# Gate and branch products with tokens on partitions, and a new order at the two ends of a two-block network

## The chip, the cores and the metric

The kernel runs on one core of a Trainium2 chip. The metric is device time in microseconds, from start to end of one execution. Three runs of the kernel before gave 2169.39, 2167.85 and 2166.99 us; their median is 2167.85 us. Beside them there is one execution recorded by the hardware profiler.

The core has five engines with queues of their own: TensorE (PE in the profile; its weight loads are PEld), VectorE (DVE), ScalarE (ACT), GpSimd (POOL) and SyncE (SP), which here issues most DMA transfers. Products land in PSUM; everything else that engines work on lies in SBUF.

## The reference

256 tokens of width 1024 pass through a first block and then through two layers of a second one. All is float32. What matters here, in short:

```python
# block 1
proj = rmsnorm(x) @ w_in                       # q, f, i, g, attention q, k, v, gates
y_hg = hgrn2_mix(...) @ w_branch_hg            # 1024 x 1024
y_at = moba_attention(...) @ w_branch_attn     # 1024 x 1024
gates = sigmoid(gl.reshape(B, S, 2, D))
merged = gates[:, :, 0] * y_hg + gates[:, :, 1] * y_at
x = x + merged @ w_out
x = x + (silu(h2 @ w_gate) * (h2 @ w_up)) @ w_down

# block 2, two layers (the first with a dense feed-forward, the second with 8 experts, top 2)
z = xn @ w_in[layer]
gates = sigmoid(z[..., OFF_GATE:].reshape(b_, s_, 4, D))
merged = (gates[:, :, 0] * (y_a @ w_branch_pool)    # 256 x 1024
          + gates[:, :, 1] * (y_b @ w_branch_conv)  # 256 x 1024
          + gates[:, :, 2] * (y_c @ w_branch_sgu)   # 256 x 1024
          + gates[:, :, 3] * (y_d @ w_branch_attn)) # 512 x 1024
h = h + merged @ w_out
```

## The kernel before

**Products.** A float32 operand is split into a rounded part `hi` and the rest `lo` (both fp32r), and a product is made of three matmuls, hi x hi, hi x lo and lo x hi. Weights come from HBM in `raw` buffers (seven of 128x2048). A *piece* is a part of a buffer with up to 1024 columns per partition; `look_ahead` (L383) copies it to `hi` on ACT, and the subtraction that gives `lo` (L408) is issued on DVE one unit later. Three pieces are split ahead (`LOOK`), with four buffers each for `hi` and `lo`.

**Units and side work.** `unit` (L460) is the step by which everything is ordered. It calls the generators of side work once (`stage`), issues the products of one piece, calls `look_ahead`, then `flush` (which issues the evacuation left by the unit before, and deferred work), and calls the same generators a second time (`finish`). So a side generator makes two calls per unit; only the first `width` of the list `sides` are served. `drain` serves side work without products between. The order on each engine is the order of the calls.

**Layouts.** `chunk_t` (L497) computes 256 output columns with the weights as stationary operand and the 256 tokens as moving one: output columns on partitions, 256 columns per matmul. `chunk_wide` (L549) has the activations as stationary operand and 512 weight columns as the moving one: tokens on partitions, two token halves `t`, 512 columns per matmul.

**Gates and branches of block 1.** Eight `chunk_t` give the gates (`evac_gate`, L842: DVE scales by the norm). Then, for each of eight groups of 128 output columns, there are two units of 24 matmuls (`o` with w_branch_hg, `att` with w_branch_attn), and `evac_merge` (L851) multiplies by the gate, adds the two and calls `merge_split` (L867), which splits the sum into the `hi` and `lo` operand `merged` of w_out.

**Gates and branches of a mixer.** The attention (`diff`, two chains of side work), `sgu`, `pool` and `conv` run as side work while 16 `chunk_t` compute the gates (L1334). `drain` (L1337) ends them all. Then, per group of 128 output columns, come a unit with w_branch_attn (12 matmuls) and one with the three smaller branches (18 matmuls). `evac_merge` (L1340) multiplies two pages of gates by the products on DVE; for the first six groups POOL makes the two additions, for the last two DVE. `merge_split` follows one or two units later.

**After them.** `residual` (L874) multiplies `merged` by w_out; its first chunk is `chunk_late` (L506), which leaves the last two of eight row groups to the end, since `merged` comes last there. The second layer goes to `moe` (L1370) instead, whose products with w_out begin with `chunk_tok_pair` (L567).

**Weights.** `plan_all` (L351) lists all pieces in order. `fill` (L367) issues loads on SP as buffers come free. Entries marked `RAW` use a raw buffer; `ANY` may also take four pages of the pool of 50 pages of 128x512, as many as `room` allows (in mixer 1 set to `ROOM_MERGE` ahead of the branches).

**PSUM.** There are two pools of four banks: `psg` for the main products (`gp`) and `pss` for side work (`sp`).

**The two ends.** `first_chunk` (L639) loads the input and the first weights in eight steps and multiplies at once. `overflow` (L1540) is a second pass over the experts for the case that one expert has more than 128 tokens; here it isn't entered. It is a conditional block at the end of the program, in which every engine branches:

```python
with self.tc.If(self.n_longest > P, preferred_fallthrough_block=False):
```

With `True` the body is to be placed next in the program, with `False` the other arm, and without the argument the compiler selects.

Of the kernel before, what the change touches and what calls it, by code (L numbers as in the profile page):

```python
# [126 lines left out]
class Net:  # L127
# [160 lines left out]
    def plan_block1(self):  # L288
# [15 lines left out]
        for c in range(8):  # L304
            yield from t(7168, c)
        for c in range(4):
            yield RAW
            p0 = self.load(a["w_branch_hg"][0], 0, 8, 256 * c, 256)
            yield RAW
            p1 = self.load(a["w_branch_attn"][0], 0, 8, 256 * c, 256)  # L310
            for m in range(2):
                yield p0[:, :, m * P:m * P + P], m
                yield p1[:, :, m * P:m * P + P], m
# [4 lines left out]
    def plan_mixer(self, l):  # L318
# [8 lines left out]
        for c in range(4):  # L327
            for b in range(4):
                yield from self.plan_t(w, 3072 + 1024 * b + 256 * c, 8)
        for c in range(4):  # L330
            yield RAW
            v = self.load(a["w_branch_attn_2"][l], 0, 4, 256 * c, 256)
            yield RAW
            raw = self.rawp.tile([P, 2048], F32, tag="raw", name=self.nm("raw"))[:, :1536].rearrange("p (k c) -> p k c", k=6)
            for i, nme in enumerate(("w_branch_pool_2", "w_branch_conv_2", "w_branch_sgu_2")):
                self.nc.sync.dma_start(raw[:, 2 * i:2 * i + 2, :], a[nme][l][:, 256 * c:256 * c + 256].rearrange("(k p) c -> p k c", p=P))
            for m in range(2):
                yield v[:, :, m * P:m * P + P], m
                yield raw[:, :, m * P:m * P + P], m
# [208 lines left out]

    def chunk_wide(self, x, evacs, width=1):  # L549

        mm = self.nc.tensor.matmul
        ps = [[self.gp() for _ in range(2)] for _ in evacs]

        def products(ps, hi, lo, r):
            for t in range(2):
                s = slice(t * P, t * P + P)
                for k in range(2):
                    xh, xl = self.xb(x, r + k)
                    mm(ps[t], xh[:, s], hi[:, k, :], start=r + k == 0, stop=False)  # L559
                    mm(ps[t], xl[:, s], hi[:, k, :], start=False, stop=False)  # L560
                    mm(ps[t], xh[:, s], lo[:, k, :], start=False, stop=r + k == 7)  # L561
        for q in range(0, 8, 4):
            for p, evac in zip(ps, evacs):
                for r in (q, q + 2):
                    self.unit(lambda hi, lo: products(p, hi, lo, r), (lambda p=p, evac=evac: evac(p)) if r == 6 else None, width)

    def chunk_tok_pair(self, x, evacs, width=1):  # L567

        ps = [[self.gp()[:, :256] for _ in range(2)] for _ in range(2)]
        for r in (0, 4):  # L570
            for i in range(2):
                self.unit(lambda hi, lo: self.mm3tok(ps[i], hi, lo, x, r),
# [66 lines left out]
    def first_chunk(self, N, xr, evac):  # L639
# [4 lines left out]
        for i in range(4):  # L644
            nc.sync.dma_start(self.x[i], xr[i])
            v = w[2 * P * i:2 * P * i + 2 * P, 1024:1536].rearrange("(k p) c -> p k c", p=P)
            for k in range(2):
                (nc.sync if i + k else nc.scalar).dma_start(raws[i // 2][:, 2 * (i % 2) + k, :], v[:, k, :])
# [7 lines left out]
        for i in range(4):  # L656
# [25 lines left out]
    def setup(self):  # L682
        nc, a, const = self.nc, self.a, self.const
        self.params = const.tile([P, NPAR], F32, name="params")
        nc.scalar.dma_start(self.params, a["params"])
# [50 lines left out]
    def block1(self):  # L736
# [74 lines left out]
        for c in range(4):  # L811
# [16 lines left out]
            if c == 1:  # L828
                self.side(bias[1])
        aq, ak, av = [None] * 4, [None] * 4, [None] * 4  # L830
# [9 lines left out]
        gates = [self.pgv(2, T, nm="gl") for _ in range(8)]  # L840

        def evac_gate(c, ps):  # L842
            b, m = divmod(c, 4)
# [986 lines left out]
```

## Time and profile before

| | |
|---|---|
| median of three runs | 2167.85 us |
| the profiled execution, whole time | 2167.5 us |
| its span, from first to last instruction | 2165.6 us |
| instructions | 35720 |
| HBM read, written | 558.32 MB, 4.75 MB |
| branch matmuls of block 1 | from 264.6 to about 310.8 us |
| branch matmuls of mixer 0 (tile b) | from 699.8 to about 730.8 us |
| branch matmuls of mixer 1 (tile b) | from 1123.9 to about 1154.9 us |
| the experts | from about 1199 to 2157 us |

A line of a group reads: line of the source, engine, operation, output<-inputs by the program's names, form, count, and then busy time and mean, or min/median/max in ns. A line of the chain or of a timeline begins with start and length in us. `[0.83 <-DVE gt L1342]` is idle time before an instruction and what ended it. [...]

### The profile page before, as it was taken

How to read it: one execution, taken by the hardware profiler on the slowest of the kernel's cores; microseconds unless marked ns; L12 is line 12 of the kernel's file. 1: busy time of each engine (PE TensorE's matmuls, PEld its weight loads, DVE VectorE, ACT ScalarE, POOL GpSimd, SP SyncE). 2: the span in 40 equal slices, each digit the busy share in tenths (PEclk: the TensorE clock that was granted, in tenths of full speed). 3: DMA queues.
4: the chain of work that ended last, by engine and by line, in shares of the span. 5: the costliest groups of instructions: out<-in, count | busy, mean ns of one | idle time of the engine just before them, and what ended most of it. 6: DMA issues, size and time to landing. Idle time of an engine off the chain costs nothing.

```text
span 2165.6 us, 35720 instructions
## 1 busy us (share of the span) xinstructions
PE 2144.1 (99%) x13587; PEld 1938.1 (89%) x13587; DVE 1769.9 (82%) x2513; ACT 1424.0 (66%) x2015; POOL 101.0 (5%) x114
## 2 busy tenths in 40 slices
PE   9999999999999999999999999999999999999998
PEld 9988999999999999999998888888888888888886
DVE  7877766655787976557878999989999999999997
ACT  6347555444655554446555888888887888788885
POOL 0000000003000300020012000000000000000100
PEclk9999999999999999999999999999999999999999
DMA  9444466646543755474548799999999999999994
GB/s 346 141 136 156 130 193 185 186 159 222 192 157 110 230 186 171 160 243 156 166 132 306 274 323 387 364 357 379 369 377 367 384 374 385 345 383 371 387 386 168
DMA packets 368275, 565.48 MB, mean 261 GB/s; under 512 B 14378, under 2 KB 177210, under 8 KB 368096
## 3 DMA queue, kind: packets, MB, share of 16 engines
q1 hardware_dynamic: 363600, 551.50, 73.4%
q0 software_dynamic: 4064, 11.05, 1.4%
q8 instruction: 108, 1.77, 0.3%
q14 instruction: 71, 0.58, 0.1%
q10 hardware_dynamic: 432, 0.57, 0.1%
HBM read 558.32 MB, written 4.75 MB: 260 GB/s over the span
## 4 chain that ended last, share of the span: by engine, by line
PE 95%; DVE 2%; DMA 1%; issue 0%; SPq 0%; ACT 0%; ACTq 0%; DVEq 0%
PE g L493 13%; PE g L494 13%; PE g L495 13%; PE g L1656 9%; PE g L1658 9%; PE g L1657 9%; PE y L1679 5%; PE y L1680 5%; PE y L1681 5%; PE g L559 2%; PE g L561 2%; PE g L560 2%; PE lev L990 1%; PE at L1636 1%; DVE lo L408 1%; PE xe L1575 1%
## 5 line engine op out<-in xcount | busy, mean ns | idle before, releaser
L185 ACT ACTIVATE hi<-raw 128x1024 fp32r<-128x1024 f32 (+2 forms) x1236 | 1125.7, 927 | 582.7 <-PE g L494 278.4
L408 DVE TENSOR_TENSOR lo<-raw,hi 128x1024 fp32r<-128x1024 f32 (+1 forms) x1228 | 1282.0, 1071 | 205.4 <-ACT hi L185 170.9
L493 PE MATMUL g<-nh,hi 128*128 128x256 f32 x1664 | 476.7, 286 | 0.0
L494 PE MATMUL g<-nl,hi 128*128 128x256 f32 x1664 | 471.1, 283 | 0.0
L495 PE MATMUL g<-nh,lo 128*128 128x256 f32 x1664 | 471.1, 283 | 0.0
L1656 PE MATMUL g<-hi,xe 128*128 128x512 f32 x896 | 354.0, 395 | 0.0
L1658 PE MATMUL g<-lo,xe 128*128 128x512 f32 x896 | 349.5, 390 | 0.0
L1657 PE MATMUL g<-hi,xe 128*128 128x512 f32 x896 | 349.2, 390 | 0.0
L493 PEld LDWEIGHTS g<-nh,hi 128*128 128x128 f32 x1664 | 319.2, 192 | 3.4 <-issue 2.3
L494 PEld LDWEIGHTS g<-nl,hi 128*128 128x128 f32 x1664 | 319.4, 192 | 0.3
L495 PEld LDWEIGHTS g<-nh,lo 128*128 128x128 f32 x1664 | 319.2, 192 | 0.0
L1658 PEld LDWEIGHTS g<-lo,xe 128*128 128x128 f32 x896 | 168.2, 188 | 35.8
L1657 PEld LDWEIGHTS g<-hi,xe 128*128 128x128 f32 x896 | 168.5, 188 | 33.4
L1656 PEld LDWEIGHTS g<-hi,xe 128*128 128x128 f32 x896 | 168.4, 188 | 33.4
L1679 PE MATMUL y<-hi,ah 128*128 128x512 f32 x448 | 175.9, 393 | 0.0
L1680 PE MATMUL y<-hi,al 128*128 128x512 f32 x448 | 174.6, 390 | 0.0
L1681 PE MATMUL y<-lo,ah 128*128 128x512 f32 x448 | 174.5, 390 | 0.0
L1681 PEld LDWEIGHTS y<-lo,ah 128*128 128x128 f32 x448 | 84.1, 188 | 17.7
L495 PE MATMUL g<-ah,lo 128*128 128x256 f32 x352 | 99.7, 283 | 0.0
L493 PE MATMUL g<-ah,hi 128*128 128x256 f32 x352 | 99.7, 283 | 0.0
L494 PE MATMUL g<-al,hi 128*128 128x256 f32 x352 | 99.7, 283 | 0.0
L1679 PEld LDWEIGHTS y<-hi,ah 128*128 128x128 f32 x448 | 84.2, 188 | 16.6
(427 smaller groups left out, 2809.3 us busy)
## 6 DMA issues: line engine op xcount, KB each, us to landing
raw<-in_moe_w_gate_up_dram SPq DMA_DIRECT2D x168, 1024.0 KB, 7.0
raw<-in_w_in_dram SPq DMA_DIRECT2D x90, 1024.0 KB, 5.2
raw<-in_moe_w_down_dram SPq DMA_DIRECT2D x88, 1024.0 KB, 6.1
raw<-in_moe_w_gate_up_dram SPq DMA_DIRECT2D x224, 256.0 KB, 7.3
raw<-in_moe_w_down_dram SPq DMA_DIRECT2D x96, 256.0 KB, 7.0
raw<-in_ffn_w_gate_up_dram SPq DMA_DIRECT2D x22, 1024.0 KB, 5.2
raw<-in_w_ffn_gate_dram SPq DMA_DIRECT2D x11, 1024.0 KB, 5.4
raw<-in_w_ffn_up_dram SPq DMA_DIRECT2D x11, 1024.0 KB, 5.3
```

The lines of the kernel that those rows point to most:

```text
L185: return self.nc.scalar.activation(out, in_, func, **kw)
L408: self.nc.vector.tensor_sub(l, x, h)
L493: mm(out, hi[:, k, :], xh, start=r + k == 0, stop=False)
L494: mm(out, hi[:, k, :], xl, start=False, stop=False)
L495: mm(out, lo[:, k, :], xh, start=False, stop=r + k == kb - 1)
L559: mm(ps[t], xh[:, s], hi[:, k, :], start=r + k == 0, stop=False)
L1656: mm(ps, xh, hi[:, k, :], start=first, stop=False)
L1657: mm(ps, xl, hi[:, k, :], start=False, stop=False)
L1658: mm(ps, xh, lo[:, k, :], start=False, stop=last)
L1679: mm(py, xh, hi[:, i, :], start=k == 0, stop=False)
L1680: mm(py, xl, hi[:, i, :], start=False, stop=False)
L1681: mm(py, xh, lo[:, i, :], start=False, stop=k == KE - 1)
```

## The change

Gates and branches are computed by `chunk_wide` or in its manner (`products_tok`), 512 output columns at a time. The gates are scaled on ACT while they leave PSUM. Products are multiplied and added on DVE (`gated`) with tokens on partitions; the sum is transposed on PE (`turn`) and split from PSUM (`merge`, `merge_now`). In block 1 the order is gates, then branches by halves of the columns. In a mixer, six of the eight wide gate chunks come first; the other two (gates 2 and 3 of the second half) are cut into half chunks and put between the branches of the first half. `sgu`, `pool` and `conv` go to the front of the side work. The last branch's multiplication is issued at once, and its merge inside the first products with w_out (`between`, `chunk_late_pair`, `chunk_tok_pair`). The loads follow the new order.

At the start, the first weight load leads ACT's queue ahead of `params`, `x[0]` is loaded in halves, later weights in one transfer of two row groups, and the first `hi` copy goes to DVE. At the end, `preferred_fallthrough_block` is left out.

```diff
 def plan_block1(self):
-        for c in range(8):
-            yield from t(7168, c)
...
+            yield from self.plan_wide(w, [7168 + 512 * (c // 2) + 1024 * (c % 2)])
+        for c in range(2):
+            for nme in ("w_branch_hg", "w_branch_attn"):
+                yield from self.plan_wide(a[nme][0], [512 * c])
 def plan_mixer(self, l):
...
+        gates = [[g for b in range(4) for g in self.plan_loads(w, 3072 + 1024 * b + 512 * c)] for c in range(2)]
+        branches = [self.plan_branches(l, c) for c in range(2)]
+        for g in gates[0] + gates[1][:5] + [branches[0][0], gates[1][5], branches[0][1], gates[1][6], branches[0][2], gates[1][7]] + branches[1]:
+            yield from g
...
+    def products_tok(self, ps, hi, lo, x, r, kb):
+        mm = self.nc.tensor.matmul
+        for t in range(2):
+            s = slice(t * P, t * P + P)
+            for k in range(2):
+                xh, xl = self.xb(x, r + k)
+                mm(ps[t], xh[:, s], hi[:, k, :], start=r + k == 0, stop=False)
+                mm(ps[t], xl[:, s], hi[:, k, :], start=False, stop=False)
+                mm(ps[t], xh[:, s], lo[:, k, :], start=False, stop=r + k == kb - 1)
+
+    def chunk_late_pair(self, x, evacs, between):
+        ps = [self.gp()[:, :T] for _ in range(4)]
+        late = []
+        for i in range(4):
+            if i == 2:
+                between()
+            run = self.stage(1)
+            late.append(self.ahead.pop(0))
+            self.mm3t(ps[i], *late[i], x, 0, 4, 8)
+            if i == 0:
+                self.look_ahead()
+            elif i == 1:
+                self.rest()
+                self.rest = lambda: None
+            self.flush()
+            self.finish(run)
+        for i, (hi, lo) in enumerate(late):
+            self.mm3t(ps[i], hi[:, 4:, :], lo[:, 4:, :], x, 4, 4, 8)
+            self.look_ahead()
+            self.flush()
+            if i % 2:
+                self.pending.append(lambda i=i: evacs[i // 2](ps[i - 1:i + 1]))
...
 def first_chunk(self, N, xr, evac):
         for i in range(4):
-            nc.sync.dma_start(self.x[i], xr[i])
             v = w[2 * P * i:2 * P * i + 2 * P, 1024:1536].rearrange("(k p) c -> p k c", p=P)
+            dst = raws[i // 2][:, 2 * (i % 2):2 * (i % 2) + 2, :]
+            if i:
+                nc.sync.dma_start(self.x[i], xr[i])
+                nc.sync.dma_start(dst, v)
+                continue
             for k in range(2):
-                (nc.sync if i + k else nc.scalar).dma_start(raws[i // 2][:, 2 * (i % 2) + k, :], v[:, k, :])
+                nc.sync.dma_start(self.x[i][:, k, :], xr[i][:, k, :])
+                (nc.sync if k else nc.scalar).dma_start(dst[:, k, :], v[:, k, :])
+        nc.scalar.dma_start(self.params, self.a["params"])
...
-                self.copy(hi[:, k, :], v[:, k, :])
+                if i + k:
+                    self.copy(hi[:, k, :], v[:, k, :])
+                else:
+                    nc.vector.tensor_copy(hi[:, k, :], v[:, k, :])
...
+    def evac_gate(self, gates, c, ps, N, func=AF.Copy):
+        gates[c] = [self.pg(nm="gt") for _ in range(2)]
+        for t, g in enumerate(gates[c]):
+            self.act(g, ps[t], func, scale=N.col[:, t:t + 1])
+
+    def gated(self, gates, b, c, ps):
+        for t in range(2):
+            g = gates[b][c][t]
+            self.nc.vector.tensor_mul(g, g, ps[t])
+            if b != self.first_branch:
+                s = gates[self.first_branch][c][t]
+                self.nc.vector.tensor_add(s, s, g)
+
+    def evac_branch(self, gates, b, c, ps, merged):
+        self.gated(gates, b, c, ps)
+        if b == self.last_branch:
+            self.side(self.merge(gates, c, merged), front=True)
+
+    def turn(self, gates, c, j):
+        pt = self.sp("mt").rearrange("p (k t) -> p k t", k=2)
+        for t in range(2):
+            y = gates[self.first_branch][c][t]
+            for k in range(2):
+                self.nc.tensor.transpose(pt[:, k, t * P:t * P + P], y[:, (2 * j + k) * P:(2 * j + k) * P + P], self.ident)
+        return pt
...
+    def merge_now(self, gates, c, merged):
+        pts = [self.turn(gates, c, j) for j in range(2)]
+        for j, pt in enumerate(pts):
+            hi, lo = merged[2 * c + j] = tuple(self.pgv(2, T, dt=F32R, nm="m" + s) for s in "hl")
+            self.copy(hi, pt)
+            self.nc.vector.tensor_sub(lo, pt, hi)
...
 def mixer(self, l, N, S):
+        for b in range(4):
+            self.chunk_wide(N.x, [lambda ps, b=b: self.evac_gate(gates[b], 0, ps, N)], width=2)
+        for b in range(2):
+            self.chunk_wide(N.x, [lambda ps, b=b: self.evac_gate(gates[b], 1, ps, N)], width=2)
+        self.drain(gens=small)
+        todo = [(b, 0) for b in range(4)] + [(b, 1) for b in range(2)]
+
+        def gate_half(b, r, width=2):
+            if r == 0:
+                late[b] = [self.gp() for _ in range(2)]
+            for q in (r, r + 2):
+                self.unit(lambda hi, lo: self.products_tok(late[b], hi, lo, N.x, q, 8),
+                          (lambda: self.evac_gate(gates[b], 1, late[b], N, AF.Sigmoid)) if q == 6 else None, width)
...
+        def branch(b, c, evac=True):
+            x = (ya, yb, yc, yd)[b]
+            ps = [self.gp() for _ in range(2)]
+            n = 4 if b == 3 else 2
+            for r in range(0, n, 2):
+                self.unit(lambda hi, lo: self.products_tok(ps, hi, lo, x, r, n),
+                          (lambda: self.evac_branch(gates, b, c, ps, merged)) if evac and r == n - 2 else None)
+            return ps
...
+        gate_half(2, 0)
+        self.drain()
+        sigmoids(2)
+        branch(0, 0)
+        sigmoids(1)
+        branch(1, 0)
+        gate_half(2, 4, 1)
+        sigmoids(1)
+        branch(2, 0)
+        gate_half(3, 0, 1)
+        sigmoids(1)
+        branch(3, 0)
+        gate_half(3, 4, 1)
+        sigmoids(1)
+        for b in range(3):
+            branch(b, 1)
+        ps = branch(3, 1, False)
+        self.flush()
+        self.gated(gates, 3, 1, ps)
+        return merged, lambda: self.merge_now(gates, 1, merged)
...
 def overflow(self):
-        with self.tc.If(self.n_longest > P, preferred_fallthrough_block=False):
+        with self.tc.If(self.n_longest > P):
```

`sigmoids(n)` applies the sigmoid on ACT to the two pages of each of the next n entries of `todo`. `merge` does what `merge_now` does, as side work.

More of the change, by code (lines that the diff above doesn't have):

```diff
@@ L571, in chunk_tok_pair @@
             for i in range(2):
+                if r == 0 and i == 1:
+                    between()
                 self.unit(lambda hi, lo: self.mm3tok(ps[i], hi, lo, x, r),
@@ L862, in block1 @@
-        self.flush(True)
-        N = self.residual(merged, 8, self.par("g_ffn", 8))
+        for c in range(2):
+            for b, x in enumerate((o, att)):
+                for g in gates[b][c]:
+                    self.act(g, g, AF.Sigmoid)
+                ps = [self.gp() for _ in range(2)]
+                for r in range(0, 8, 2):
+                    last = r == 6 and not (b and c)
+                    self.unit(lambda hi, lo: self.products_tok(ps, hi, lo, x, r, 8),
+                              (lambda b=b, c=c, ps=ps: self.evac_branch(gates, b, c, ps, merged)) if last else None)
@@ new lines, in merge @@
+    def merge(self, gates, c, merged):
+        for j in range(2):
+            yield 1
+            yield 1
+            pt = self.turn(gates, c, j)
+            yield 1
+            hi, lo = merged[2 * c + j] = tuple(self.pgv(2, T, dt=F32R, nm="m" + s) for s in "hl")
+            self.copy(hi, pt)
+            self.defer(lambda pt=pt, hi=hi, lo=lo: self.nc.vector.tensor_sub(lo, pt, hi))
+            yield 1
+    def merge_now(self, gates, c, merged):
+        pts = [self.turn(gates, c, j) for j in range(2)]
+        for j, pt in enumerate(pts):
+            hi, lo = merged[2 * c + j] = tuple(self.pgv(2, T, dt=F32R, nm="m" + s) for s in "hl")
+            self.copy(hi, pt)
+            self.nc.vector.tensor_sub(lo, pt, hi)
@@ new lines, in mixer, with sigmoids @@
+        self.drain(gens=small)
[6 more added lines that the diff above has]
+                          (lambda: self.evac_gate(gates[b], 1, late[b], N, AF.Sigmoid)) if q == 6 else None, width)
+        def sigmoids(n):
+            for _ in range(n):
+                if todo:
+                    b, c = todo.pop(0)
+                    for g in gates[b][c]:
+                        self.act(g, g, AF.Sigmoid)
@@ L1352, in mixer @@
+        def branch(b, c, evac=True):
+            x = (ya, yb, yc, yd)[b]
+            ps = [self.gp() for _ in range(2)]
+            n = 4 if b == 3 else 2
[3 more added lines that the diff above has]
+            return ps
+        late = {}
         if l:
@@ L1414, in moe @@
         evacs = [lambda ps, c=c: evac(c, ps) for c in range(4)]
[L1415 removed]
+        self.chunk_tok_pair(merged, evacs[:2], between, width=4)
         for c in range(2, 4):
@@ L1758, in run @@
             self.side(st)
-            merged = self.mixer(0, N, S)
-            N = self.residual(merged, 8, self.par(("n2", 0), 8))
+            merged, between = self.mixer(0, N, S)
+            N = self.residual(merged, 8, self.par(("n2", 0), 8), between)
             N = self.ffn(N, self.par(("n1", 1), 8))
@@ L1765, in run @@
             self.side(self.res_tok())
-            merged = self.mixer(1, N, S)
-            self.moe(merged)
+            merged, between = self.mixer(1, N, S)
+            self.moe(merged, between)
             self.overflow()
```

139 lines of the change are left out of this document (40 added, 99 removed).

## The prediction

> **What bounds the kernel now.** I read the head of the page first, then the chain that ended last, then windows of single stages.
>
> ```profile
> PE 2144.1 (99%) x13587; PEld 1938.1 (89%) x13587; DVE 1769.9 (82%) x2513; ACT 1424.0 (66%) x2015; POOL 101.0 (5%) x114
> PEclk9999999999999999999999999999999999999999
> PE 95%; DVE 2%; DMA 1%; issue 0%; SPq 0%; ACT 0%; ACTq 0%; DVEq 0%
> ```
>
> TensorE's clock is granted throughout, and the chain is PE for 95%. So an edit is worth what it does to the count and spacing of products, to the few places where PE is starved, or to the two ends. PE's busy share hides short gaps, because products overlap; gaps are found by counting products in a window. In these rows the second number is the length in us, and after it stand busy us and count of each engine:
>
> ```profile
> 264.60:310.90 46.30, 46.30 (x388) 46.30 (x387) 29.54 (x38) 25.84 (x33) 0.00 (x0) 1.00 0.61 195
> 346.00:526.00 180.00, 180.00 (x1496) 179.84 (x1497) 111.32 (x121) 83.56 (x96) 12.84 (x17) 1.00 0.59 187
> 699.96:739.90 39.94, 35.91 (x290) 34.86 (x288) 38.50 (x48) 23.68 (x41) 16.56 (x12) 1.00 0.74 231
> 1124.00:1161.00 37.00, 33.10 (x269) 32.23 (x268) 35.68 (x45) 22.22 (x41) 16.59 (x12) 1.00 0.97 330
> ```
>
> The second row, 1496 products of 256 columns in 180 us, gives 0.120 us each. The first is the branch stage of block 1: 388 x 0.120 = 46.6, so PE never waits there. Rows three and four are the branch stages of the two mixers with the first products after them: 290 x 0.120 = 34.8 of 39.9 us, and 269 x 0.120 = 32.3 of 37.0. PE loses 5.1 and 4.7 us. The 55 longest pieces of the chain say to whom, and the groups of tile gt, at 690 to 745 us, say why (min/median/max ns):
>
> ```profile
> 714.60 1.44 DVE ml L872
> 719.17 1.51 DVE ml L872
> 723.90 1.43 DVE ml L872
> 728.54 1.43 DVE ml L872
> L872 DVE TENSOR_TENSOR ml<-gt,mh x8: 418/1510/1522, 709.9 to 738.4; 128x256 fp32r<-128x256 f32 x8
> L1345 POOL TENSOR_TENSOR gt<-gt,gt x6: 1887/1914/1942, 705.4 to 727.8; 128x512 f32<-128x512 f32 x6
> L1342 DVE TENSOR_TENSOR gt<-gt,b x8: 673/675/680, 704.0 to 735.4; 128x512 f32<-128x512 f32 x8
> L1345 DVE TENSOR_TENSOR gt<-gt,gt x2: 691/692/693, 732.9 to 736.7; 128x512 f32<-128x512 f32 x2
> L185 ACT ACTIVATE gt<-gt x16: 611/616/632, 698.9 to 722.2; 128x512 f32<-128x512 f32 x16
> PE b L493 <- DVE gt L1342: 3.3, 4, 0.8
> ```
>
> One output column of 128 takes 4.65 us ((728.54 - 714.60)/3) where its 30 products take 3.6. DVE is the bound: the subtraction ml takes 1.51 us while POOL adds, 0.42 without. PE then waits for the multiplication L1342 that must free its PSUM bank.
>
> **The change part by part.** First the wider products. Two stretches of the old 512-wide stages, in the projections (0.2267 = 1.36/6) and in the experts, where four transposes stand between:
>
> ```profile
> 171.41 0.39 PE L561 MATMUL g<-lo,nh 128*128 128x512 f32 x1
> 172.77 0.39 PE L561 MATMUL g<-lo,nh 128*128 128x512 f32 x1
> ...
> 1341.43 0.60 PE L1636 MATMUL at<-consts,s 128*128 128x128 f32 x4
> 1341.78 0.48 PE L1656 MATMUL g<-hi,xe 128*128 128x512 f32 x1
> 1342.10 0.40 PE L1657 MATMUL g<-hi,xe 128*128 128x512 f32 x1
> ```
>
> A pair of 256-wide products (0.2400) becomes one of 512 (0.2267): 0.0133 us less. Block 1 has 8 gate chunks x 48 + 8 columns x 48 = 768 products, hence 384 pairs: -5.1 us. A mixer has 16 x 48 + 8 x 30 = 1008, 504 pairs: -6.7 us, twice. All three stages together -18.5.
>
> [...]
>
> With tokens on partitions, the merged rows must be turned back: 16 transposes per stage, in 4 groups of 4. The group above costs 1342.10 - 1341.43 - 0.2267 = 0.44 us. 4 x 0.44 = +1.8 us per stage, all on PE's path.
>
> Gate evacuation moves from DVE to ACT; both have room while gates run (ACT 66%, DVE 82% over the span), so I cost it at nothing. If ACT were late, the next weight half would be late; three pieces are split ahead, 8 us of PE work.
>
> Next the stalls of the mixers. The POOL additions go, so ml's 1.51 goes with them; -5.1 and -4.7 us. What is late next? DVE gets the additions. In the last five units (12 products, 12 x 0.2267 = 2.72 us of PE each) a branch costs DVE up to two multiplications and two additions beside one weight subtraction:
>
> ```profile
> L408 DVE TENSOR_TENSOR lo<-raw,hi 128x1024 fp32r<-128x1024 f32 x844 | 1025.7, 1228 | 180.0 <-ACT hi L185 147.6
> L185 ACT ACTIVATE hi<-raw 128x1024 fp32r<-128x1024 f32 x844 | 891.6, 1060 | 506.4 <-PE g L494 241.3 <-PE g L560 73.4 <-PE g L1657 71.1
> 697.61 1.28 ACT L180 ACT_TABLE_LOAD   x1
> 698.90 2.19 ACT L185 ACTIVATE gt<-gt 128x512 f32<-128x512 f32 x4
> L960 PE MATMUL fl<-consts,yd x8: 272/272/273, 627.5 to 664.2; 128*128 128x128 f32 x8
> ```
>
> 1.23 + 2 x 0.675 + 2 x 0.69 = 3.96 us against 2.72. But the first of the five (branch 0) adds nothing (2.58), the two late gate units before them give DVE only 1.23 each, and the last branch has two units. Adding up the queue from there, the last addition ends some 1.8 us after the last branch product; PE first has two half chunks of w_out (2 x 12 x 0.120 = 2.9 us), then transposes. The second half of the merge is split while PE does the other two half chunks. So nothing, with about 1 us to spare.
>
> The first branches are worse off. gate_half(2, 0) holds two of the four PSUM banks of psg until its second half, branch(0, 0) takes the other two, and branch(1, 0) needs two more. They come free only when DVE has multiplied branch 0, and that call comes in flush, behind the subtraction of a weight piece whose hi copy stands on ACT behind a table load and four sigmoids (1.28 + 2.19). Let T be the start of branch(0, 0). ACT's last hi copy of the gates ends at T - 2.1, the two copies of the last attention page (0.67 + 0.6) at T - 0.9, table and sigmoids at T + 2.5, the hi copy at T + 3.5, DVE's subtraction at T + 4.7, the first multiplication at T + 5.4. PE is ready at T + 2.7: +2.7 us per mixer. Its bounds are 0, if these copies and sigmoids run a unit earlier, and 2.7 + 2.5 = 5.2 if the hi copy waits for the sigmoids of the next branch too. I take 2.7.
>
> The chains of the attention must end before drain: in before, its last transposes stand at 664.2, some 35 us ahead of the branches at 699.8. A diff chain has 44 calls, 22 units. Now pool, conv and sgu go in front of it and take 9 places, and 24 + 2 gate units come before drain instead of 32. By my count of calls unit 26 finishes all but two calls, which issue nothing for PE: 0 us, without reserve.
>
> The weights: each stage still loads 1 MB per two units, in rows twice as long, through the same seven raw buffers. On SP's queue the branch loads of the first half now stand between those of the late gates, in the order of use. DMA has room in mixer 0 (share 0.74 above) and hardly any in mixer 1 (0.97), where w_out and expert pages are fetched ahead; there the last branch load is issued some 16 units before w_out is used, earlier than now, so I take nothing.
>
> **The two ends.** The start, with the chain of its first product:
>
> ```profile
> 0.75 0.45 ACTq L685 DMA_DIRECT2D params<-in_params_dram  x1
> 1.23 0.49 ACTq L648 DMA_DIRECT2D raw<-in_w_in_dram  x1
> 4.11 0.51 ACT L185 ACTIVATE nh<-x,params 128x256 fp32r<-128x256 f32 x1 [1.07 <-DMA x<-in_xT_dram]
> 5.36 0.63 ACT L185 ACTIVATE hi<-raw 128x512 fp32r<-128x512 f32 x1 [0.75 <-DMA raw<-in_w_in_dram]
> 6.04 0.55 PE L670 MATMUL g<-nh,hi 128*128 128x256 f32 x1 [0.34 <-ACT hi L185]
> params<-in_params_dram ACTq DMA_DIRECT2D x1, 48.5 KB, 3.1
> ```
>
> The weight half goes out 0.48 us earlier; params then land near 1.23 + 3.1 = 4.3, nh ends at 4.9, when the weights arrive. The hi copy on DVE costs about what ACT takes. First product near 5.5: -0.5 us (bounds +0.3, if params are late, to -0.6). SP issues 9 transfers instead of 11; one more stands ahead of the second weight half, which PE needs only 1.4 us later.
>
> The end. Rows of L1543 (the If) and L1826 (the close), and the last output:
>
> ```profile
> L1543 SPq EVENT_SEMAPHORE  x8: 17/17/17, 2157.8 to 2160.8; - x8
> L1543 PEldq COMPARE_BRANCH  x2: 95/1953/3811, 2155.3 to 2156.2; - x2
> L1543 SPq COMPARE_BRANCH  x2: 38/46/53, 2157.7 to 2160.8; - x2
> L1826 SPq EVENT_SEMAPHORE  x14: 17/28/28, 2163.7 to 2165.6; - x14
> out_dram<-acc SPq DMA_DIRECT2D x1, 256.0 KB, 3.5
> ```
>
> SP branches at 2157.7, waits for the output's landing until 2160.8, branches again over the unused body, and its next instruction stands at 2163.7: 2.9 us after the jump. If leaving the choice to the compiler puts the body next, the single jump comes at 2157.7 and its 2.9 us run beside the 3.5 us of the transfer; some 0.5 us of semaphore waits follow. -2.4 us; bounds 0 (same layout as now) and -2.9.
>
> **The sum.** Block 1: -5.1 + 1.8 = -3.3. Mixers: 2 x (-6.7 + 1.8 + 2.7) - 9.8 = -14.2. Ends -0.5 - 2.4. Together -20.4. The profiled run took 2167.5 (span 2165.6 and 1.9 around it): 2147.1. The median of the runs is 0.35 above the profiled run: **2147.5 us**.
>
> **The rivals.**
> - No new wait: the bank comes free in time. For it: ACT idles 506 us ahead of hi copies, so the sigmoids may start earlier. 2147.5 - 5.4 = 2142. Against: the order of the queues is written out.
> - DVE becomes the bound at the end of the mixers, and the jump pays nothing: three units with 3.96 - 2.72 = 1.24 us too much, unbuffered, are 3.7 us per mixer: 2147.5 + 7.4 = 2155, with the tail 2157. For it: DVE is at 38.5 of 39.9 us in that stage now.
> [...]
> - Slower than before: the attention chains don't end before drain, and PE stands open. Each unit missing costs a round of copy, scale and transpose in series, from 0.67 + 0.69 = 1.4 us up to a unit, 2.7. It needs 20.4 us, so 4 to 7 units missing in each mixer; with ten at 2.0 the time is 2147.5 + 40 = 2187. Against: the count above misses one.
>
> **How the numbers follow.** Chances: forecast 0.45 (its own range 2144 to 2152), no new wait 0.2, DVE bound 0.2, narrow gain 0.04, open chains 0.05; 0.06 lies between the third and the same time. The range for 8 in 10 takes in the first three but for the tips: 2141.5 to 2157. About 0.2% (4.3 us) is what a measurement of this kernel can tell from no change: below 2163.5 is faster, 0.91; within, 0.04; slower, 0.05.
>
> **What would show it.** In the changed profile: 0.2267 us per product in the gate and branch windows; no POOL additions between gates and w_out; a wait of PE at branch(1, 0) for the multiplication of branch 0, near 2.7 us, in both mixers; the last fl of yd in the unit before that; no wait at the first transposes of mt; the first product near 5.5 us; SP's first instruction of the close about 4.0 us after its output's issue rather than 6.4. The prediction is wrong if the sum of gaps in a mixer's branch stage is over 6 us or the chain there shows DVE.

## The result, and the profile after

The changed kernel takes 2152.07 us (median of four runs, 2151.04 to 2153.13) beside 2167.51 us before (2166.99 to 2169.39): a ratio of 0.9928, 95% interval 0.9916 to 0.9940. The time is 4.6 us above the forecast. It lies in the range given for 8 in 10 (2141.5 to 2157) and 0.07 us outside the forecast's own (2144 to 2152). The profiled execution took 2152.17 us, span 2150.4; before it was 2167.5 and 2165.6.

The page of the changed kernel: busy time by engine, the granted clock in 40 slices, and the chain by engine.

```profile
PE 2134.0 (99%) x12243; PEld 1870.0 (87%) x12243; DVE 1736.9 (81%) x2424; ACT 1436.6 (67%) x2022; POOL 67.9 (3%) x90
PEclk9999999999999999999999999999999999999999
PE 97%; ACT 1%; DMA 1%; DVE 0%; issue 0%; SPq 0%; DVEq 0%
```

Products went from 13587 to 12243. DVE's 2% of the chain are gone, and ACT's share went from 0% to 1%. The clock row still says 9 everywhere, though it dropped twice: a slice is 54 us wide, too coarse for 3 us at half speed. Landmarks on PE say where the time went (starts of the first product of each kind, us):

| | before | after | difference |
|---|---|---|---|
| first product | 6.04 | 5.51 | -0.53 |
| first 512-wide product (projections) | 37.06 | 37.19 | +0.13 |
| block 1, first branch product | 264.68 | 262.82 | -1.86 |
| block 1, first product with w_out | 310.84 | 307.44 | -3.40 |
| block 1, first product of the norm behind w_out (tile ms) | 339.64 | 337.14 | -2.50 |
| mixer 0, first product with w_out | 732.40 | 725.22 | -7.18 |
| mixer 0, first product of the norm behind w_out (tile ms) | 762.89 | 754.93 | -7.96 |
| mixer 1, first product with w_out | 1156.57 | 1144.39 | -12.18 |
| mixer 1, first product of the routing behind w_out (tile pos) | 1189.38 | 1176.84 | -12.54 |
| last product | 2155.64 | 2143.09 | -12.55 |
| end of the span | 2165.6 | 2150.4 | -15.2 |

Every gain was made in the stages that were changed; the dense layers and the experts neither add nor lose. Windows of the changed kernel (length; then busy us and count of PE, PEld, DVE, ACT, POOL; granted clock, DMA share, GB/s): the three branch stages, then the seam between branch 0 and branch 1 in mixer 0, the products behind it, the stretch after these, and the products behind the same seam in mixer 1.

```profile
262.82:307.44 44.62, 44.62 (x204) 36.91 (x202) 27.45 (x29) 23.93 (x29) 0.00 (x0) 1.00 0.55 177
676.30:725.22 48.92, 46.27 (x201) 37.87 (x200) 36.02 (x43) 26.80 (x36) 0.00 (x0) 0.97 0.53 174
1094.95:1144.39 49.44, 46.63 (x201) 37.82 (x200) 36.01 (x45) 28.36 (x40) 0.00 (x0) 0.97 0.85 291
678.90:681.80 2.90, 0.28 (x2) 0.00 (x0) 1.93 (x3) 2.90 (x4) 0.00 (x0) 0.97 0.00 0
681.84:684.96 3.12, 3.12 (x8) 2.47 (x8) 1.77 (x3) 0.00 (x0) 0.00 (x0) 0.50 0.80 266
684.96:690.00 5.04, 5.04 (x23) 4.17 (x22) 3.75 (x6) 2.19 (x3) 0.00 (x0) 0.99 0.76 255
1100.50:1104.50 4.00, 4.00 (x12) 3.15 (x13) 2.96 (x4) 0.00 (x0) 0.00 (x0) 0.62 0.94 295
```

About the same count of products takes 44.6 us in block 1 and 48.9 and 49.4 us in the mixers. Part of the difference is the forecast wait: nothing runs on PE from 678.9 to 681.8. The rest was not forecast: behind the wait eight products take 3.12 us, under a granted clock of 0.50, and only then is the clock full again. The row of the wait also shows DMA share 0.00: by the program a raw buffer comes free only after DVE's subtraction, which waits here.

The queues at the seam of mixer 0; branch 0 starts at T = 676.30. First ACT's timeline of the changed kernel (start, length, line, operation):

```profile
673.08 1.06 ACT L185 ACTIVATE hi<-raw 128x1024 fp32r<-128x1024 f32 x1 [0.85 <-PE g L566]
674.05 0.67 ACT L185 ACTIVATE qk<-fl,gs 128x512 f32<-128x512 f32 x1
674.75 0.63 ACT L185 ACTIVATE ydh<-qk 128x512 fp32r<-128x512 f32 x1
675.40 1.28 ACT L180 ACT_TABLE_LOAD   x1
676.69 2.19 ACT L185 ACTIVATE gt<-gt 128x512 f32<-128x512 f32 x4
678.79 1.04 ACT L185 ACTIVATE hi<-raw 128x1024 fp32r<-128x1024 f32 x1
```

Then DVE's:

```profile
679.87 1.23 DVE L417 TENSOR_TENSOR lo<-raw,hi 128x1024 fp32r<-128x1024 f32 x1 [2.63 <-ACT hi L185]
681.01 1.28 DVE L916 TENSOR_TENSOR gt<-gt,g 128x512 f32<-128x512 f32 x2
```

And PE's:

```profile
678.80 0.39 PE L567 MATMUL g<-lo,yah 128*128 128x512 f32 x1
681.84 0.77 PE L565 MATMUL g<-hi,ybh 128*128 128x512 f32 x1 [2.65 <-ACT hi L185]
682.40 0.63 PE L566 MATMUL g<-hi,ybl 128*128 128x512 f32 x1
682.83 0.63 PE L567 MATMUL g<-lo,ybh 128*128 128x512 f32 x1
```

The sigmoids end at T + 2.6, the hi copy at T + 3.5, the subtraction at T + 4.8, half of the two multiplications at T + 5.35, and PE goes on at T + 5.5. Products are counted from start to start: ahead of the wait each is recorded as 0.39 us long and begins 0.227 us behind the one before. From one start to the next, 681.84 - 678.80 = 3.04 us, 2.81 more than a product's 0.227. The releaser named in the brackets is ACT's hi copy, which began the chain; what ended it is shown below by the runs. After the wait the starts are 0.43 us apart.

At the end of the program, the rows of the If (L1642) and the close (L1925) on SP's queue:

```profile
L1642 SPq EVENT_SEMAPHORE  x8: 17/17/17, 2148.2 to 2148.7; - x8
L1642 SPq COMPARE_BRANCH  x1: 50/50/50, 2145.1 to 2145.1; - x1
...
L1925 SPq EVENT_SEMAPHORE  x14: 17/28/28, 2148.8 to 2150.3; - x14
```

SP branches once, at 2145.1, and its close follows the semaphores directly. The output was issued at 2144.73, so the close comes 4.1 us behind it; before it was 6.4.

### The profile page after: what moved, and what is told of

Same layout as the page of the kernel before. It is cut to its first block, busy times and chain, and to the rows that moved or that the text cites. A ratio compares the mean times of both kernels' runs of the same rounds, so it can differ in the third digit from the quotient of the medians.

```text
span 2150.4 us, 32906 instructions
## 1 busy us (share of the span) xinstructions
PE 2134.0 (99%) x12243; PEld 1870.0 (87%) x12243; DVE 1736.9 (81%) x2424; ACT 1436.6 (67%) x2022; POOL 67.9 (3%) x90
## 4 chain that ended last, share of the span: by engine, by line
PE 97%; ACT 1%; DMA 1%; DVE 0%; issue 0%; SPq 0%; DVEq 0%; ACTq 0%
PE g L1755 9%; PE g L1757 9%; PE g L1756 9%; PE g L502 8%; PE g L503 8%; PE g L504 8%; PE g L565 7%; PE g L566 7%; PE g L567 7%; PE y L1778 5%; PE y L1779 5%; PE y L1780 5%; PE lev L1069 1%; PE at L1735 1%; PE xe L1674 1%; PE g L554 1%
## 5 line engine op out<-in xcount | busy, mean ns | idle before, releaser
L417 DVE TENSOR_TENSOR lo<-raw,hi 128x1024 fp32r<-128x1024 f32 (+2 forms) x1216 | 1273.5, 1074 | 237.5 <-ACT hi L185 202.4
L502 PE MATMUL g<-nh,hi 128*128 128x256 f32 x1024 | 291.7, 285 | 0.0
L504 PE MATMUL g<-nh,lo 128*128 128x256 f32 x1024 | 289.8, 283 | 0.0
L503 PE MATMUL g<-nl,hi 128*128 128x256 f32 x1024 | 289.7, 283 | 0.0
L565 PE MATMUL g<-hi,nh 128*128 128x512 f32 x544 | 219.6, 404 | 0.2 <-DVE gt L916 0.2
L567 PE MATMUL g<-lo,nh 128*128 128x512 f32 x544 | 212.4, 390 | 0.0
L566 PE MATMUL g<-hi,nl 128*128 128x512 f32 x544 | 212.0, 390 | 0.0
L503 PEld LDWEIGHTS g<-nl,hi 128*128 128x128 f32 x1024 | 196.5, 192 | 0.2
L502 PEld LDWEIGHTS g<-nh,hi 128*128 128x128 f32 x1024 | 196.4, 192 | 0.2
L504 PEld LDWEIGHTS g<-nh,lo 128*128 128x128 f32 x1024 | 196.4, 192 | 0.0
```

The source lines that it names most:

```text
L417: self.nc.vector.tensor_sub(l, x, h)
L502: mm(out, hi[:, k, :], xh, start=r + k == 0, stop=False)
L503: mm(out, hi[:, k, :], xl, start=False, stop=False)
L504: mm(out, lo[:, k, :], xh, start=False, stop=r + k == kb - 1)
```

## The experiments

"Changed kernel" is the kernel after. A time given without a range is of one execution.

**Sigmoids earlier.** Does the place of table load and sigmoids make the wait?

```diff
+        sigmoids(2)
         gate_half(2, 0)
         self.drain()
-        sigmoids(2)
         branch(0, 0)
```

> One line moved: the first two sigmoid calls (table load and four pages on ACT) stand before the half chunk of gate 2 instead of after it. Queue theory: PE's 2.81 us at branch(1, 0) is a wait for a PSUM bank that DVE frees late, because its multiplication stands behind a weight subtraction whose hi copy stands behind these sigmoids. Then the hi copy ends near T + 1.1 (T: start of branch(0, 0)), the subtraction near T + 2.3, the first multiplication near T + 3.0, and 0.3 to 0.4 us of the wait is left. The eight or so products after the wait, at 0.427 us each instead of 0.227 with the granted clock at 0.50, come from the pause and go with it (1.5 us). Together some 4 us per mixer, 8 us in all against the changed kernel: 2144. Rival (the pause comes from the weights, since the DMA share is 0.00 in it, or from another wait): the wait stays near 2.8 us and the time near 2152.

2151.88 us (four runs, 2149.86 to 2152.61): no difference. The wait is 2.64 and 2.63 us. ACT's timeline of this kernel:

```profile
671.44 1.28 ACT L180 ACT_TABLE_LOAD   x1
672.74 2.19 ACT L185 ACTIVATE gt<-gt 128x512 f32<-128x512 f32 x4
674.83 1.99 ACT L185 ACTIVATE hi<-raw 128x1024 fp32r<-128x1024 f32 x2
676.73 0.67 ACT L185 ACTIVATE qk<-fl,gs 128x512 f32<-128x512 f32 x1
677.43 0.63 ACT L185 ACTIVATE ydh<-qk 128x512 fp32r<-128x512 f32 x1
677.97 1.04 ACT L185 ACTIVATE hi<-raw 128x1024 fp32r<-128x1024 f32 x1
```

The expectation failed. The sigmoids run 4 us sooner, but what they overtook (two hi copies, the last attention pages) piles up behind them, and the decisive hi copy moves only from 678.79 to 677.97. DVE then makes two subtractions in a row and multiplies at 680.98, not 681.01. This suggests that the sum of ACT's work ahead of that copy counts, not its order; the next run takes some of it away.

**Half the sigmoids later.** Less work ahead of the copy.

```diff
-        sigmoids(2)
+        sigmoids(1)
         branch(0, 0)
-        sigmoids(1)
+        sigmoids(2)
         branch(1, 0)
```

> One pair of sigmoids (two pages, 1.04 us on ACT) is moved from before branch(0, 0) to after it. Queue theory: the hi copy, the subtraction and the multiplication come 1.04 us sooner, so the wait falls from 2.81 to about 1.8 us in both mixers. Rival (the wait doesn't hang on the sigmoids): it stays at 2.8. Clock: if a pause of 1.8 us is short enough, the slow products go too; if not, they stay at 0.427 us. Both are open.

2146.92 us, 5.2 less. The wait is 1.78 us in both mixers. Windows of this kernel, the wait and the products behind it, in mixer 0 and in mixer 1:

```profile
678.87:680.60 1.73, 0.29 (x2) 0.00 (x0) 1.73 (x3) 1.73 (x4) 0.00 (x0) 1.00 0.00 0
680.70:684.00 3.30, 3.22 (x14) 2.73 (x15) 2.66 (x4) 1.54 (x3) 0.00 (x0) 1.00 0.89 277
1094.97:1096.70 1.73, 0.29 (x2) 0.00 (x0) 1.73 (x3) 1.73 (x4) 0.00 (x0) 1.00 0.00 0
1096.80:1100.10 3.30, 3.22 (x14) 2.73 (x15) 2.66 (x4) 1.54 (x3) 0.00 (x0) 1.00 0.88 264
```

Two pages of sigmoids less ahead of the copy shorten the wait by 1.03 us, and in this execution the clock stays at 1.00 behind it (by an estimate in the last section another might have lost it). The waits account for 2.06 of the 5.2 us, the products behind them for 3.1.

**Keeping PE busy in the wait.** Twelve products that nobody reads, in mixer 1 only, between branch 0 and branch 1:

```diff
         sigmoids(1)
+        if l:
+            self.warm(12, N.x[0][0])
         branch(1, 0)
```

> In mixer 1 alone, twelve products whose result nobody reads (512 columns, 12 x 0.227 = 2.7 us) fill PE's time between branch(0, 0) and branch(1, 0); mixer 0 is as in the changed kernel. Clock theory: the products of branch(1, 0) are slow because PE stood still for 2.8 us. Then in mixer 1 they run at 0.227 us with the granted clock at 1.00, and branch(1, 0) ends 1.6 us sooner after its start, while mixer 0 still shows 0.427 us. Rival (they are slow because ACT, DVE or the DMA transfers hinder them at that time): 0.427 us in both mixers.

2150.22 us. Windows of this kernel: the products behind the wait in mixer 0, then the whole stage of mixer 1.

```profile
681.70:684.70 3.00, 3.00 (x7) 2.42 (x8) 1.65 (x3) 0.00 (x0) 0.00 (x0) 0.50 0.78 267
1094.80:1142.62 47.82, 47.66 (x215) 38.93 (x214) 35.96 (x45) 28.37 (x40) 0.00 (x0) 1.00 0.88 302
```

Mixer 0, untouched, has the slow products. Mixer 1 has none, its clock is 1.00, and its stage takes 47.82 instead of 49.44 us, 1.62 less, though branch 1 starts no sooner: 5.54 us behind branch 0, as in the changed kernel. So the slow products are the clock's answer to an idle array, not contention with the DMA traffic that sets in again at that moment.

**A fifth PSUM bank.** Is it the bank that branch 1 waits for?

```diff
-        self.psg = ctx.enter_context(tc.tile_pool(name="psg", bufs=4, space=PSUM))
-        self.pss = ctx.enter_context(tc.tile_pool(name="pss", bufs=4, space=PSUM))
+        self.psg = ctx.enter_context(tc.tile_pool(name="psg", bufs=5, space=PSUM))
+        self.pss = ctx.enter_context(tc.tile_pool(name="pss", bufs=3, space=PSUM))
```

> The changed kernel with five PSUM banks for the main products and three for side work, instead of four and four. Theory (branch 1 waits for a PSUM bank): its first token half has a bank now, so PE waits only ahead of the second token half, six products later: 2.81 - 6 x 0.2267 = 1.45 us instead of 2.81 in both mixers, and the products behind it run at 0.227; 2 x (1.36 + 1.5) = 5.7 us less if three banks do for the side work: 2146.4 us. Rival (PE waits for the lo operand, not for a bank): the wait stays at 2.8 us ahead of the first product of branch 1, 2152 us.

PE's timeline of this kernel:

```profile
685.17 0.39 PE L567 MATMUL g<-lo,ybh 128*128 128x512 f32 x1
686.76 0.50 PE L565 MATMUL g<-hi,ybh 128*128 128x512 f32 x1 [1.20 <-DVE gt L916]
```

The first six products of branch 1 run at once; PE then waits 1.36 us in both mixers, near the 1.45 reckoned, and the releaser is now the multiplication (L916). Two of these six products read lo, so lo was there, and the wait is one for the bank. The time, 2157.96 us, is worse by 5.9: with three banks the side work of the attention falls behind (one gap of 2.86 us at 622, and mixer 0 reaches its branches at 681.32 instead of 676.30). The mean granted clock from 594 us to the branches, with that gap in it, was 0.98; in the changed kernel it was 1.00 from 590 us to the branches. The part of the expectation that depended on three banks being enough failed.

**Another order.** If the bank is the cause, two units of other work between branch 0 and the next taker of its banks cover the multiplication.

```diff
         self.drain()
-        sigmoids(2)
+        sigmoids(1)
         branch(0, 0)
         sigmoids(1)
-        branch(1, 0)
         gate_half(2, 4, 1)
-        sigmoids(1)
+        branch(1, 0)
         branch(2, 0)
+        sigmoids(1)
         gate_half(3, 0, 1)
         sigmoids(1)
         branch(3, 0)
+        sigmoids(1)
         gate_half(3, 4, 1)
...
```

Left out above: the branch weights are grouped as pool alone, then conv with sgu, and the later weights of the start come in two transfers.

> The changed kernel with the first half of a mixer in another order: branch 0, second half of gate 2, branch 1, branch 2, first half of gate 3, branch 3, second half of gate 3. The sigmoids stand one pair ahead of each branch or gate half, and the later weights of the start come in two transfers each. Theory (branch 1 waits because its PSUM bank comes free only by the multiplication of branch 0, which stands in the queues behind table load, sigmoids, hi copy and subtraction; two units of PE work between them cover it): no wait of PE over 0.4 us in either branch stage, so no products of 0.427 us behind it, and 2 x (2.8 + 1.5) = 8.7 us less than the changed kernel; the start gives 0.5 more: 2152.07 - 9.2 = 2142.9 us, 2141 to 2145. Rival (DVE as a whole is late in this stage, so the wait only moves to the next branch): a wait of 1 to 3 us ahead of branch 2 or branch 3, and 2146 to 2150 us.

2142.95 us (four runs, 2142.47 to 2144.06): a ratio of 0.9887 to before, interval 0.9871 to 0.9904, and 9.1 us less than the changed kernel. Windows of the branch stages of this kernel:

```profile
677.25:721.73 44.48, 44.48 (x201) 36.82 (x200) 35.73 (x43) 26.81 (x36) 0.00 (x0) 1.00 0.57 190
1091.47:1136.39 44.92, 44.77 (x201) 36.74 (x200) 35.74 (x45) 28.36 (x40) 0.00 (x0) 1.00 0.92 320
```

The stages fall from 48.92 and 49.44 to 44.48 and 44.92, 8.96 together, to the length of block 1's. One wait of 0.31 us is left in mixer 1. The rival, DVE late as a whole, is out: DVE does about the same work, 35.7 us instead of 36.0, and PE doesn't wait. The order isn't the only thing that differs from the changed kernel: this run, like the one with half the sigmoids later, has one pair of sigmoids ahead of branch 0. Against that run's 2146.92 us, the new order is worth some 4.0 us, which is about the two waits of 1.78 us.

**Cutting the products again.**

```diff
+        def mm(out, a, w, start, stop):
+            cut = (slice(0, 256), slice(256, 512)) if self.narrow and not (start or stop) else (slice(0, 512),)
+            for c in cut:
+                self.nc.tensor.matmul(out[:, c], a, w[:, c], start=start, stop=stop)
...
```

Left out above: `narrow` is set around the gates and branches of the three stages.

> The changed kernel with the gate and branch products cut back to 256 columns: all but the first and the last product of each accumulation, 1232 products in all, become two of 256 columns each. Theory (a product of 256 columns takes 0.120 to 0.121 us and one of 512 takes 0.2287 on average, so each pair costs 0.0117 us more): +14.4 us, 2166.5 us, with 16.4 if the 0.0133 of the prediction were right. [...]

2165.90 us (2164.24 to 2167.89): +13.8 us, or 13.8/1232 = 0.0112 us per cut. By stages of the traces, gates and branches of block 1 grow by 2.07 (0.18 of it from a later end of the start) and 2.24, those of mixer 0 by 3.46 and 1.69, of mixer 1 by 3.43 and 1.35: 14.24, or 0.0116. Block 1's branch stage in this kernel:

```profile
264.89:311.75 46.86, 46.86 (x379) 46.12 (x378) 27.57 (x29) 23.91 (x29) 0.00 (x0) 1.00 0.53 173
```

46.86 against 44.62 with the clock at 1.00 in both: 2.24/176 = 0.0127. The gain comes from the width, at 0.011 to 0.013 us a pair. The row has 378 weight loads (PEld) for 379 products, so the second half of a cut pair loads its weights again; width and number of loads were not told apart.

**The old tail.**

```diff
-        with self.tc.If(self.n_longest > P):
+        with self.tc.If(self.n_longest > P, preferred_fallthrough_block=False):
```

> The changed kernel with the argument of the conditional block as before the change. Theory (the layout alone sets what follows the last output's issue): the stretch from the last product to the end grows from 7.3 to 9.96 us, +2.65, and SP's first instruction of the close stands 2.9 us behind the one that waits for the output: 2154.7 us. Rival (the stretch shrank because something else comes earlier): it stays at 7.3 us, 2152 us.

The rows of L1642 and L1925 on SP's queue:

```profile
L1642 SPq EVENT_SEMAPHORE  x8: 17/17/17, 2143.8 to 2147.0; - x8
...
L1642 SPq COMPARE_BRANCH  x2: 38/46/53, 2143.7 to 2147.1; - x2
```

```profile
L1925 SPq EVENT_SEMAPHORE  x14: 17/28/28, 2149.8 to 2151.3; - x14
```

From the last product (2141.64) to the end of the span are 9.76 us instead of 7.3, and SP again branches twice, with 2.7 us behind the second branch. Nothing else was changed, so the layout is the cause. The time, 2153.19 us, is only 1.1 above the changed kernel's, since mixer 0 met no slow products in this execution, by these windows (mixer 0, then mixer 1):

```profile
681.90:684.90 3.00, 2.97 (x13) 2.49 (x14) 2.88 (x4) 0.17 (x2) 0.00 (x0) 1.00 0.90 266
...
1099.10:1103.40 4.30, 4.30 (x13) 3.41 (x14) 2.95 (x4) 0.31 (x1) 0.00 (x0) 0.64 0.82 295
```

Both mixers waited 2.81 us. The one whose clock held had its stage done in 47.43 us (676.39 to 723.82) instead of 48.92.

**The start, three ways.** In the changed kernel PE stops again at 8.5 us. Its timeline there, of ACT and then of PE:

```profile
8.44 0.63 ACT L185 ACTIVATE hi<-raw 128x512 fp32r<-128x512 f32 x1 [1.60 <-DMA raw<-in_w_in_dram]
...
9.12 0.51 PE L715 MATMUL g<-nh,hi 128*128 128x256 f32 x2 [0.32 <-ACT hi L185]
```

The second part of the weights, now one transfer, isn't there yet. First two transfers, with the sigmoids of the first experiment:

```diff
-                nc.sync.dma_start(dst, v)
+                for k in range(2):
+                    nc.sync.dma_start(dst[:, k, :], v[:, k, :])
                 continue
```

> The moved sigmoids together with the start's later weight loads in two transfers each again. If both theories hold: 2144 less 0.5 us, 2143.5. If only one of the two edits works, 2144 or 2151.5.

2150.74 us (five runs, 2148.12 to 2152.12), 1.3 less than the changed kernel, with a spread of 4.0 us. The stop at 8.5 is gone here, but mixer 1 also kept its clock in the profiled execution, so this run doesn't separate the two. Then, with the other order of branches (`g1_alternate` is that run above), the whole old start, and the changed kernel's start:

> The order of g1_alternate with the start as it was before the change: params first on ACT's queue, x in whole loads, the first hi copy on ACT. The first product was 0.5 us earlier in the changed kernel, but its first 512-wide product was not (37.19 against 37.06 us). Theory (the weights of the later row groups set the pace of the first 37 us, so the new start only moves a wait): first product near 6.0, first 512-wide product at 36.9 to 37.4 us, and the time equal to that of the new start within 0.7 us, 2142.5 to 2143.5. Rival (the step of the prediction: -0.5 us from the start): 0.5 us slower than with the new start, first 512-wide product 0.5 us later.

> The order of g1_alternate with the start of the changed kernel (later weights of the start in one transfer each). Both branch stages as in g1_alternate: no wait over 0.4 us. Theory (start pays nothing either way): 2142.5 to 2143.5 us, equal to h1_old_start. Rival (one large transfer lands late and costs 0.5 us): 2143.4 us, first 512-wide product 0.5 us later than with two transfers; the two profiles of two transfers had it at 37.01 and 38.16, those of one transfer at 37.15 to 37.37.

2142.77 us (2142.68 to 2143.93) with the old start, 2143.22 (2142.64 to 2143.59) with the changed one, 2142.95 with two transfers. First 512-wide product at 36.77, 37.14 and 38.16 us (the last in the slowest of its four runs), first product at 5.92, 5.35 and 5.36. The new start makes the first product earlier, and nothing behind it: the stop at 8.5 us, for weights that land later, takes the gain back.

**The old stalls.** In the kernel before, all additions on DVE:

```diff
-            e = nc.gpsimd if m < 6 else nc.vector
+            e = nc.vector
```

> The kernel before, with the additions that POOL made in the branch stages of the mixers put on DVE. Theory (DVE is the bound of a column: subtractions 0.954 + 0.707, two multiplications 1.35, two additions 1.38, merge 0.42 make 4.8 us without POOL, against 4.65 with it): the stalls stay, 1 to 1.6 us per column behind the 3.6 us of its products, and the time is within 2 us of before, 2166 to 2169.5. Rival (the slowing of DVE by POOL's additions is the cause by itself, and what DVE has left besides fits into 3.6 us): the stalls go, -9.8 us, 2158 us.

2162.68 us, 4.5 less than before (2167.16 us beside it): neither theory. The groups of this kernel in the branch stage of mixer 0:

```profile
L1342 DVE TENSOR_TENSOR gt<-gt,b x8: 677/679/681, 703.9 to 733.1; 128x512 f32<-128x512 f32 x8
...
L872 DVE TENSOR_TENSOR ml<-gt,mh x8: 417/417/424, 711.0 to 736.0; 128x256 fp32r<-128x256 f32 x8
```

Without POOL's additions ml takes 0.42 us instead of 1.51. A column takes (733.1 - 703.9)/7 = 4.17 us; the same row before gives (735.4 - 704.0)/7 = 4.49. That is still more than the 3.6 us of its products, and DVE has no idle time over 0.15 us from the second column on, so DVE stays the bound; the stage shrinks by 2.2 of some 5 us in each mixer. So the old stalls had two shares: POOL's slowing of DVE, and DVE's own work.

## Why the prediction was right, and where its sizes were off

Direction and mechanism were right; the gain was put 5.2 us too high. By steps, in us, from the landmarks:

| step | forecast | measured |
|---|---|---|
| block 1 | -3.3 | -2.6 (from 37 us to the norm behind w_out) |
| mixers | -14.2 | -10.04 (-5.46 and -4.58) |
| start | -0.5 | +0.1 |
| tail | -2.4 | -2.65 |
| sum | -20.4 | -15.2 (whole time -15.3) |

- **Width.** The mechanism holds, the size was too large. The forecast had 0.0133 us per pair; cutting the products again gave 0.0116. For 1392 pairs that is 16.1 instead of 18.5: 2.4 us short. (With the 0.0127 of block 1's branch stage it would be 17.7, 0.8 us short.) The forecast took its 0.2267 from six products; the branch window of block 1 averages 0.2287, the products right behind transposes included. A narrow gain of the width, given 0.04, fell with these figures.
- **Transposes.** +1.8 a stage was right. Their group in the changed kernel has 48 = 3 x 16, as listed; a group of four stands in the chain with 0.44 us.

```profile
L932 PE MATMUL mt<-consts,gt x48: 270/272/273, 290.2 to 1148.0; 128*128 128x128 f32 x48
```

- **The new wait.** Place, cause and length were right: 2.81 us in both mixers against 2.7, for the bank of branch 0, and the queue from the sigmoids to the multiplication ran within 0.1 us of the forecast's T + 2.5, 3.5, 4.7 and 5.4. **Its price was wrong.** "+2.7 us per mixer" counted the idle time alone and put the products behind it at nothing. They ran at half clock: 0.34 + 6 x 0.20 = 1.5 us in mixer 0 and 8 x 0.20 = 1.6 in mixer 1. This is the step of the sum that failed most, 3.1 us, and the run with unread products shows it by itself (1.62).
- **Old stalls.** They went whole, as forecast; the layout leaves POOL out and gives DVE less to do per output. Behind the new wait one gap of 0.31 us in mixer 1 is all that is left of waiting before w_out, and the first transposes of mt don't wait, so the rival of DVE as the bound at the end of the mixers fell.
- **Chains of the attention.** The last fl of yd stands at 673.4 us, in the unit before branch 0 at 676.30, as counted. "Without reserve" was no figure of speech: one bank less made these chains late.
- **Start.** The step was wrong. First product -0.53 as forecast (its hi copy took 0.43 us on DVE, 0.63 on ACT before), but a stop behind it took that back; the forecast followed the chain to the first product and not to the next transfer.
- **Tail.** Right in mechanism and size; the close is 4.1 us behind the output's issue (forecast 4.0).

Width 2.4, clock 3.1, wait 0.2, start 0.6, less 0.25 of the tail make 6.0 us, and 5.2 were missing. The 0.8 us between them isn't settled; it is less than the two sizes of the width differ by. The rival without a new wait was put at 2142, and the order that removes the wait gave 2142.95. Since width and start were put too high in that sum as well, some of this nearness is luck.

## What to carry to other kernels

Price a pause of TensorE with what follows it: here nine of eleven pauses of 2.6 to 2.8 us cost up to 1.6 us more in slow products, and by an estimate from the windows of the last section (3.41 us less the 1.98 busy us behind which the clock held) a pause of up to about 1.4 us loses no clock wherever it falls. Where two steps in a row share PSUM banks, follow the bank through every queue that must run before it is free. Taking work out of that queue helped here, moving it forward in the same queue did not, and units of other work between the two steps removed the rest of the wait. An earlier first product is worth nothing until the next transfers have been followed as well.

## What the hardware showed that was not expected

**In these traces the clock falls by windows of 3.41 us, and a window needn't be idle throughout.** Over these runs PE paused 2.57 to 2.81 us ahead of branch 1 eleven times: in nine the granted clock fell to 0.50 behind it, and products of 512 columns stood 0.427 us apart instead of 0.227; in two it stayed at 1.00. Two pauses of 1.78 us and one of 1.36 left it at 1.00.

The traces tell the two outcomes apart. In the changed kernel the two stretches of half clock between products last 3.41 us each and start at 681.62 and 1101.46 us, 123 times 3.413 apart; the third, behind the last product, starts at 2145.94, 429 times 3.413 behind the first. So the clock can be read window by window. One execution, that of the moved sigmoids with the start in two transfers, has both outcomes with pauses of 2.64 us. Its windows along this grid are the pause of mixer 0 and the window behind it, then the pause of mixer 1 in two windows and the one behind them:

```profile
678.97:682.38 3.41, 0.94 (x5) 0.79 (x5) 3.41 (x5) 1.71 (x3) 0.00 (x0) 1.00 0.38 97
682.38:685.79 3.41, 3.41 (x10) 2.63 (x9) 2.07 (x3) 0.00 (x0) 0.00 (x0) 0.50 1.01 379
1095.39:1098.80 3.41, 2.20 (x10) 1.50 (x8) 2.45 (x4) 3.38 (x6) 0.00 (x0) 1.00 0.44 152
1098.80:1102.21 3.41, 2.14 (x9) 1.80 (x10) 3.34 (x5) 0.47 (x1) 0.00 (x0) 1.00 0.45 135
1102.21:1105.62 3.41, 3.41 (x16) 2.82 (x15) 3.34 (x5) 1.08 (x2) 0.00 (x0) 1.00 1.03 371
```

In mixer 0 the pause lies in one window; PE is busy 0.94 of its 3.41 us, and the next window has half the clock. In mixer 1 an equal pause is shared by two windows with 2.20 and 2.14 us busy, and the clock holds. The changed kernel and the one before agree, read in the same way. In the changed kernel the windows ahead of the slow products (from 678.21 and 1098.05 us) have 0.97 us busy each, and the least busy one behind which the clock stayed at 1.00 (from 1220.93) has 2.35. In the kernel before, the clock was 0.50 behind a window with 1.94 us busy (from 2153.41, with the last products) and 1.00 behind one with 1.98 (from 1153.30). By this the pauses of 1.78 us held by their place: in one window such a pause, 1.62 us between the recorded ends and starts, would leave 1.79 us busy and drop the clock, so each must have been shared by two windows (an estimate from these figures). The twelve unread products were not lucky in this way: their window, 1097.70 to 1101.11, is busy throughout, and with the pause in it about 0.9 us would be left (an estimate: branch 1 starts at 1100.21).

**POOL's additions made DVE's subtraction ml take 3.6 times as long** (1.51 instead of 0.42 us), and taking them to DVE, which then has more instructions, saves 4.5 us in one execution. The kernel before shows where the time goes: the slow subtraction ends just behind an addition that was already running when it began.

```profile
709.16 1.94 POOL L1345 TENSOR_TENSOR gt<-gt,gt 128x512 f32<-128x512 f32 x1 [0.68 <-DVE gt L1343]
709.87 1.51 DVE L872 TENSOR_TENSOR ml<-gt,mh 128x256 fp32r<-128x256 f32 x1
```

ml begins inside the addition and ends 0.28 us behind it (711.38 and 711.10); all ten slow ones of the two mixers end 0.27 to 0.29 us behind such an addition. In the same stretch the subtraction lo of 128x768 that began at 705.23, before POOL's addition of 705.41, took 0.95 us, as it does without POOL's additions, and the multiplication at 707.81, which reads one operand from PSUM, took 0.68 us in the midst of POOL's work (707.41 to 708.48), as elsewhere. So it isn't DVE as a whole that was slower.
